# Modulation rows of a two-block transformer: loads on another queue, products in pairs, three vectors in other stages

## The chip, the cores and the metric

The kernel runs on one core of one Trainium2 chip. The metric is the device time of one execution in microseconds (us), as the median of several runs. A profile is one execution, recorded by the hardware.

## The reference

One launch computes two transformer blocks in a row on 256 tokens of width 1024, in float32. The first block has two layers, each with a mixer (differential attention and a gated recurrence in layer 0, attention in layer 1), layer norms, a feed-forward of width 4096 and a gated side input. The second block has two layers that are conditioned on a vector c, and carries a second stream of 256 context tokens with its own conditioning vector. For each of its layers six modulation vectors are computed for both streams, and they scale, shift and gate the normalised activations:

```
mod = (s_lat @ w_mod[i] + b_mod[i])[:, None, :]
mod_c = s_ctx @ w_mod[i] + b_mod[i]
sh1, sc1, g1, sh2, sc2, g2 = jnp.split(mod, 6, axis=-1)
h = rms_norm_2(x, norm_mix[i]) * (1.0 + sc1) + sh1
y, yc = token_mixers(h, hc, ...)
x = x + g1 * y
h = rms_norm_2(x, norm_ffn[i]) * (1.0 + sc2) + sh2
x = x + g2 * swiglu(h, w_gate[i], w_up[i], w_down[i])
```

Here `s_lat` and `s_ctx` are two vectors of 1024, and `w_mod[i]` is 1024 x 6144. None of this depends on the first block, so the twelve vectors (six for each of two layers, written j = 0 to 5 below) can be computed at any time before they are needed.

## The kernel before

All large weights are streamed once. `WeightStream` (L200 on) cuts them into units, mostly of 512 KB. For each unit SyncE (SP) issues a load into one of four raw buffers (L212), ACT rounds it to a high part (L214), DVE subtracts to get a low part (L216), and TensorE (PE) multiplies three times (high by high, high by low, low by high; L279 to L281 in `proj`, L825 to L827 and L850 to L852 in the feed-forwards of the first block, L1474 to L1476 in those of the second). There are four buffers for the two parts too, and a unit's load is emitted four units ahead of its use.

The program is a list of items, each a number of weight units and a function. It is put together by `weave`, which spreads one list evenly over another, and `side_by_side`, which puts side work at the ends of feed-forward groups. So side work such as the context stream and the modulation rows runs between weight products. The items are traced in this order; a scheduler then orders the instructions of each engine, by priority (the place in the program) and by a simulated time, and allots the buffers and PSUM banks. Each engine, and each queue of DMA issues, executes in that fixed order and waits at an instruction whose inputs or buffers are not ready. SP has the weight loads and most others; POOL (GpSimd) has the modulation rows, small parameters, and the reciprocal square roots of the norms (L385).

`modulation` (L938) makes one item of each quarter of a vector (`part(j, u)`, u from 0 to 3). A quarter takes two rows of 128 x 1024 of `w_mod_2`, 512 KB each. POOL issues the row's load (L952) into a buffer `fr` (two of them; `bc` for the first six rows), and PE multiplies it by the silu of the two conditioning vectors, `cT` (128 x 32, two columns of which are used), in four column groups of 32 that lie side by side in the array (L954). The eight rows of a vector accumulate in the one PSUM bank `fil`. With the last quarter DVE clears a buffer, POOL loads the bias into it, and DVE adds the sum (L962); gates are kept as they are, and the others are turned into columns by two small products (L968).

Of the kernel before, what the change touches and what calls it, by code (L numbers as in the profile page):

```python
# [119 lines left out]
def body(ctx: ExitStack, tc: tile.TileContext, A: dict, out: bass.AP):  # L120
# [29 lines left out]

    mm = nc.tensor.matmul
    V = nc.vector
    S = nc.scalar
# [114 lines left out]
    def proj(w, kdim, chunks, xs, evac, t_outer=(), tag="acc", first=0):  # L268
        new = tag if callable(tag) else lambda: PT(tag)

        items = []

        nu = kdim // 2

        def mms(o, x, wt, u):
            (xh, xl), (wh, wl) = x, wt
            for kk in range(2):
                k = 2 * ((u + first) % nu) + kk
                mm(o, xh[:, k, :], wh[:, kk, :], start=(u == 0 and kk == 0), stop=False)  # L279
                mm(o, xh[:, k, :], wl[:, kk, :], start=False, stop=False)  # L280
                mm(o, xl[:, k, :], wh[:, kk, :], start=False, stop=(u == nu - 1 and kk == 1))  # L281

        for ci, (c0, n) in enumerate(chunks):
            units = [(w, 2 * ((u + first) % nu), 2, c0, n) for u in range(nu)]
            if ci in t_outer:
                def whole(*wts, ci=ci, n=n):
                    for i, x in enumerate(xs()):
                        ps = new()[:, 0:n]
                        for u in range(nu):
                            mms(ps, x, wts[u], u)  # L290
                        evac(ci, i, ps)

                items.append((units, whole))
            else:
                held = []
                for u in range(nu):
                    def part(wt, ci=ci, n=n, u=u, held=held):
                        x = xs()
                        if u == 0:
                            held.extend(new()[:, 0:n] for _ in x)  # L300
                        for i in range(len(x)):
                            mms(held[i], x[i], wt, u)
                        if u == nu - 1:
                            for i in range(len(x)):
                                evac(ci, i, held[i])

                    items.append(([units[u]], part))
        return items

    def projT(w, kdim, c0, nb, xs, evac, tag="acc"):  # L310
# [4 lines left out]
        def part(wt, u):  # L315
# [3 lines left out]
            for kk in range(2):  # L319
                k = 2 * u + kk  # L320
                mh, ml = [m[:, k, :] for m in xT]
                for b in range(nb):
# [3 lines left out]
                    mm(o, wh[:, kk, bs], ml, start=False, stop=False, skip_group_check=True)  # L326
                    mm(o, wl[:, kk, bs], mh, start=False, stop=(k == kdim - 1), skip_group_check=True)
            if 2 * u == kdim - 2:
# [460 lines left out]
    def block1_layer(l, xT, done, side):  # L789
# [25 lines left out]
        def up_part(g, u, wt):  # L815
# [3 lines left out]
            for b in range(4):  # L819
                o = pss[g][b // 2][:, b % 2, :]  # L820
                for kk in range(2):
# [4 lines left out]
                    mm(o, wh[:, kk, bs], ml, start=False, stop=False, skip_group_check=True)  # L826
                    mm(o, wl[:, kk, bs], mh, start=False, stop=(k == 7), skip_group_check=True)  # L827
            if u == 3:
# [9 lines left out]
        def down_part(g, hs, *us):  # L838
# [3 lines left out]
            for t in range(2):  # L842
                ts_ = slice(t * P, (t + 1) * P)
                for n in range(2):
                    o = acc[g][t][n]
                    for i, h in enumerate(hs):
                        wh, wl = us[2 * i + n]
                        for kk in range(2):
                            b = 2 * h + kk
                            mm(o, hh[:, b, ts_], wh[:, kk, :], start=(b == 0), stop=False)  # L850
                            mm(o, hh[:, b, ts_], wl[:, kk, :], start=False, stop=False)  # L851
                            mm(o, hl[:, b, ts_], wh[:, kk, :], start=False, stop=(b == 3))  # L852
                    if 1 in hs:
# [84 lines left out]
    def modulation(l, box, js):  # L938
# [3 lines left out]
        def part(j, u):  # L942
# [3 lines left out]
            if u == 0:  # L946
                st[j] = PT("fil")
            ps = st[j]
            for k in (2 * u, 2 * u + 1):
                early[0] += 1  # L950
                raw = T([P, D], F32, "bc" if early[0] <= 6 else "fr", 2)
                nc.gpsimd.dma_start(raw, A["w_mod_2"][l, k * P:(k + 1) * P, j * D:(j + 1) * D])  # L952
                for g in range(4):
                    mm(ps[32 * g:32 * g + 32, 0:256], cT[:, k, :], raw[:, 256 * g:256 * g + 256],  # L954
                       start=(k == 0), stop=(k == KD - 1), tile_position=(0, 32 * g))
            if u < 3:
                return
# [461 lines left out]
    def block2_layer(l, xT, pr, box, ce, done, side):  # L1419
# [44 lines left out]
        def up_part(g, m, u, wt):  # L1464
# [3 lines left out]
            for b in range(2):  # L1468
                o = pss[g][m][:, b, :]
                bs = slice(b * P, (b + 1) * P)  # L1470
                for kk in range(4):
# [3 lines left out]
                    mm(o, wh[:, kk, bs], ml, start=False, stop=False, skip_group_check=True)  # L1475
                    mm(o, wl[:, kk, bs], mh, start=False, stop=(k == 7), skip_group_check=True)  # L1476
            if m == 1 and u == 1:
# [8 lines left out]
        def down_part(gs, *us):  # L1486
# [5 lines left out]
            for t in range(2):  # L1492
                ts_ = slice(t * P, (t + 1) * P)
                for n in range(2):
                    cs = slice(n * 512, (n + 1) * 512)
                    o = acc["y"][t][n]
                    for i, (g, (hh, hl)) in enumerate(zip(gs, hs)):
                        wh, wl = us[2 * i + n]
                        for kk in range(2):
                            mm(o, hh[:, kk, ts_], wh[:, kk, :], start=(kk == 0 and g == 0), stop=False)  # L1500
                            mm(o, hh[:, kk, ts_], wl[:, kk, :], start=False, stop=False)  # L1501
                            mm(o, hl[:, kk, ts_], wh[:, kk, :], start=False, stop=(kk == 1 and g == NG - 1))  # L1502
                    if NG - 1 in gs:
# [22 lines left out]
    def ctx_ffn(box):  # L1526
# [16 lines left out]
        def up_part(g, m, u, wt):  # L1543
# [3 lines left out]
            for b in range(2):  # L1547
                o = pss[g, m][:, b, :]
                bs = slice(b * P, (b + 1) * P)
                for kk in range(4):  # L1550
# [3 lines left out]
                    mm(o, wh[:, kk, bs], ml, start=False, stop=False, skip_group_check=True)  # L1554
                    mm(o, wl[:, kk, bs], mh, start=False, stop=(k == 7), skip_group_check=True)
            if u == 0:
# [11 lines left out]
        def down_part(g, *us):  # L1568
# [3 lines left out]
            for t in range(2):  # L1572
                ts_ = slice(t * P, (t + 1) * P)
                for n in range(2):
# [3 lines left out]
                    for kk in range(2):  # L1578
                        mm(o, h[:, 0, kk, ts_], wh[:, kk, :], start=(kk == 0), stop=False)
                        mm(o, h[:, 0, kk, ts_], wl[:, kk, :], start=False, stop=False)  # L1580
                        mm(o, h[:, 1, kk, ts_], wh[:, kk, :], start=False, stop=(kk == 1))
                    if g == 0:
# [80 lines left out]
    def mod(l, *js):  # L1663
        return modulation(l, boxes[l], js)

    program += block1_layer(0, xTs[0], to_next(1), dict(tail=flat(ctx_a[:1]), lr=4, mix=mod(0, 0, 1) + ctx_n + mod(0, 2), first=flat(ctx_a[1:2]) + mod(0, 3), ffn=ctx_a[2:-2],
                                                        end=flat(ctx_a[-2:]), last=mod(0, 4)))
    program += block1_layer(1, xTs[1], to_next(2), dict(tail=[], lr=6, mix=mod(0, 5) + mod(1, 0), first=mod(1, 1), ffn=ctx_b[:-2],
                                                        end=flat(ctx_b[-2:]), last=mod(1, 2)))
    ce1 = Stream(1)  # L1670
# [59 lines left out]
```

The twelve vectors lie in the program as follows (the calls at the end of `body`): j = 0, 1, 2 of layer 0 in the mixer of the first block's layer 0, j = 3 in the first group of its feed-forward, j = 4 at the end of that layer; j = 5, and j = 0 of layer 1, in the mixer of the first block's layer 1, j = 1 in the first group of its feed-forward, j = 2 at the end of the layer; j = 3 and 4 in the mixer of the second block's layer 1, j = 5 between its output projection (two quarters) and its feed-forward (two quarters). In the profile the mixers' last parts are found at 130 to 160 and 600 to 640, the first block ends at about 938, the second block's last mixer runs to about 1690, and its last feed-forward from 1726.

## Time and profile before

| | us |
|---|---|
| median of 3 runs | 1928.41 |
| lowest and highest | 1926.06, 1931.02 |
| profiled execution, its own time | 1929.02 |
| span of that execution in the trace | 1927.3 |

The profile gives, for each engine, its busy time and what it waited for. An engine's idle time is put down to the instruction before which it was idle, and to what ended the wait. A name such as `PE fil L954 <- DMA fr<-in_w_mod_dram` reads: TensorE, about to write `fil` at line 954, waited for the transfer into buffer `fr`. In a timeline, neighbouring instructions of one line are merged, with their count behind "x"; every float32 matmul here is two instructions, so that a row's four products are 8. PEclk is the granted share of TensorE's clock. A few matmul records can be missing.

### The profile page before, as it was taken

How to read it: one execution, taken by the hardware profiler on the slowest of the kernel's cores; microseconds unless marked ns; L12 is line 12 of the kernel's file. 1: busy time of each engine (PE TensorE's matmuls, PEld its weight loads, DVE VectorE, ACT ScalarE, POOL GpSimd, SP SyncE). 2: the span in 40 equal slices, each digit the busy share in tenths (PEclk: the TensorE clock that was granted, in tenths of full speed). 3: DMA queues.
4: the chain of work that ended last, by engine and by line, in shares of the span. 5: the costliest groups of instructions: out<-in, count | busy, mean ns of one | idle time of the engine just before them, and what ended most of it. 6: DMA issues, size and time to landing. Idle time of an engine off the chain costs nothing. (4 is left out here: it accounts for less than half of the span.)

```text
span 1927.3 us, 31895 instructions
## 1 busy us (share of the span) xinstructions
PE 1853.6 (96%) x12481; PEld 1578.1 (82%) x12481; DVE 1213.4 (63%) x2297; ACT 989.4 (51%) x1630; POOL 118.1 (6%) x194
## 2 busy tenths in 40 slices
PE   8989999999999999999899999999999999889997
PEld 5756797997887698887687998989998987669997
DVE  5564656557666666667577776676645766755555
ACT  5453465444556455553457753454646556444443
POOL 3111100000101100000000000000000000210000
PEclk9998999999999999999899999999999999899999
DMA  8744653555576554556452445556565454455553
GB/s 296 248 169 149 232 186 131 184 166 202 186 231 217 178 184 139 168 183 206 135 186 92 133 141 165 176 185 186 183 186 169 138 181 137 139 190 183 185 180 105
DMA packets 101411, 338.84 MB, mean 176 GB/s; under 512 B 12148, under 2 KB 13388, under 8 KB 101260
## 3 DMA queue, kind: packets, MB, share of 16 engines
q1 hardware_dynamic: 86124, 286.00, 46.1%
q0 software_dynamic: 15136, 50.80, 7.8%
q8 instruction: 98, 1.61, 0.3%
q14 instruction: 53, 0.43, 0.1%
HBM read 335.70 MB, written 1.05 MB: 175 GB/s over the span
## 5 line engine op out<-in xcount | busy, mean ns | idle before, releaser
L216 DVE TENSOR_TENSOR wl<-wr,wh 128x1024 fp32r<-128x1024 f32 (+3 forms) x562 | 637.9, 1137 | 398.9 <-ACT wh L214 395.9
L214 ACT CAST wh<-wr 128x1024 fp32r<-128x1024 f32 (+3 forms) x562 | 549.5, 980 | 645.3 <-PE acc L281 140.1
L279 PE MATMUL acc<-wh,mh 128*128 128x256 f32 (+3 forms) x400 | 133.0, 338 | 0.3 <-ACT mh L357 0.2
L280 PE MATMUL acc<-wl,mh 128*128 128x256 f32 (+3 forms) x400 | 131.6, 330 | 0.5 <-DVE wl L216 0.5
L281 PE MATMUL acc<-wh,ml 128*128 128x256 f32 (+3 forms) x400 | 131.2, 330 | 0.0
L280 PE MATMUL acc<-wl,xh 128*128 128x512 f32 (+3 forms) x304 | 119.3, 393 | 2.4 <-DVE wl L216 2.4
L279 PE MATMUL acc<-wh,xh 128*128 128x512 f32 (+3 forms) x304 | 117.6, 397 | 2.9 <-ACT xh L378 1.9
L281 PE MATMUL acc<-wh,xl 128*128 128x512 f32 (+3 forms) x304 | 117.1, 386 | 0.1
L850 PE MATMUL acc<-wh,a 128*128 128x512 f32 x256 | 101.9, 401 | 0.0
L852 PE MATMUL acc<-wh,a 128*128 128x512 f32 x256 | 101.3, 397 | 0.0
L851 PE MATMUL acc<-wl,a 128*128 128x512 f32 x256 | 101.3, 396 | 0.0
L1476 PE MATMUL sc<-xh,wl 128*128 128x256 f32 x352 | 99.6, 283 | 0.0
L1475 PE MATMUL sc<-xl,wh 128*128 128x256 f32 x352 | 99.5, 283 | 0.0
L1474 PE MATMUL sc<-xh,wh 128*128 128x256 f32 x352 | 99.5, 283 | 0.0
L1475 PE MATMUL sc<-ml,wh 128*128 128x256 f32 x352 | 99.2, 282 | 0.0
L1474 PE MATMUL sc<-mh,wh 128*128 128x256 f32 x352 | 98.5, 280 | 0.0
L1476 PE MATMUL sc<-mh,wl 128*128 128x256 f32 x352 | 98.4, 280 | 0.0
L952 POOL DMA_DIRECT2D fr<-in_w_mod_dram x90 | 48.8, 544 | 690.5 <-PE fil L954 563.3
L279 PEld LDWEIGHTS acc<-wh,mh 128*128 128x128 f32 x400 | 75.5, 190 | 13.7 <-issue 4.5
L954 PE MATMUL fil<-fr,cT 128*32 128x256 f32 x720 | 66.4, 415 | 19.5 <-DMA fr<-in_w_mod_dram 19.5
L280 PEld LDWEIGHTS acc<-wl,mh 128*128 128x128 f32 x400 | 75.9, 190 | 7.7 <-DVE wl L216 1.4
L281 PEld LDWEIGHTS acc<-wh,ml 128*128 128x128 f32 x400 | 75.6, 190 | 6.3 <-issue 0.6
(575 smaller groups left out, 4764.4 us busy)
## 6 DMA issues: line engine op xcount, KB each, us to landing
wr<-in_ffn_w_dram SPq DMA_DIRECT2D x128, 512.0 KB, 3.4
fr<-in_w_mod_dram POOLq DMA_DIRECT2D x90, 512.0 KB, 5.1
wr<-in_w_gate_dram SPq DMA_DIRECT2D x66, 512.0 KB, 3.9
wr<-in_w_up_dram SPq DMA_DIRECT2D x66, 512.0 KB, 4.1
wr<-in_w_down_dram SPq DMA_DIRECT2D x66, 512.0 KB, 3.6
wr<-in_w_in_dram SPq DMA_DIRECT2D x40, 384.0 KB, 3.1
wr<-in_ev_w_in_dram SPq DMA_DIRECT2D x28, 512.0 KB, 4.6
wr<-in_w_in_dram SPq DMA_DIRECT2D x28, 512.0 KB, 4.1
```

What stands on the lines that cost most here:

```text
L214: S.copy(hi, raw)
L216: V.tensor_tensor(lo, raw, hi, ALU.subtract)
L279: mm(o, xh[:, k, :], wh[:, kk, :], start=(u == 0 and kk == 0), stop=False)
L280: mm(o, xh[:, k, :], wl[:, kk, :], start=False, stop=False)
L281: mm(o, xl[:, k, :], wh[:, kk, :], start=False, stop=(u == nu - 1 and kk == 1))
L850: mm(o, hh[:, b, ts_], wh[:, kk, :], start=(b == 0), stop=False)
L851: mm(o, hh[:, b, ts_], wl[:, kk, :], start=False, stop=False)
L852: mm(o, hl[:, b, ts_], wh[:, kk, :], start=False, stop=(b == 3))
L954: mm(ps[32 * g:32 * g + 32, 0:256], cT[:, k, :], raw[:, 256 * g:256 * g + 256], start=(k == 0), stop=(k == KD - 1), tile_position=(0, 32 * g))
L1474: mm(o, wh[:, kk, bs], mh, start=(k == 0 and b == 0), stop=False, skip_group_check=True)
L1475: mm(o, wh[:, kk, bs], ml, start=False, stop=False, skip_group_check=True)
L1476: mm(o, wl[:, kk, bs], mh, start=False, stop=(k == 7), skip_group_check=True)
```

## The change

The loads of rows and biases are issued by SP in place of POOL. The two rows of a quarter are loaded first and then multiplied together: in two rounds over the four column groups, the rows alternate, so that each group gets both rows and the first product needs the second row. Each quarter is its own accumulation, which DVE adds to the bias row; the bias row is cleared and loaded with the first quarter. All dense weight products that end a triple now go through `wm`, which records the last one issued, and a quarter's products get an ordering edge behind it (`tc.issue_after`, an edge for the scheduler, not a wait on the chip). Three vectors move: j = 4 of layer 0 into the feed-forward of the first block's layer 1, j = 2 of layer 1 into that of the second block's layer 0, j = 5 of layer 1 into that of the second block's layer 1, from its fifth group of items on. The diff, without the further places at which `mm` becomes `wm`:

```
+    dense = []
+
+    def wm(*args, **kw):
+
+        dense[:] = [mm(*args, **kw).ins]
...
-                mm(o, xl[:, k, :], wh[:, kk, :], start=False, stop=(u == nu - 1 and kk == 1))
+                wm(o, xl[:, k, :], wh[:, kk, :], start=False, stop=(u == nu - 1 and kk == 1))
...
             if u == 0:
-                st[j] = PT("fil")
-            ps = st[j]
+                bm = st[j] = T([P, 256], F32, "gate" if j in (2, 5) else "bm", 3 if j in (2, 5) else 1)
+                V.memset(bm, 0.0)
+                for s in range(2):
+                    nc.sync.dma_start(bm[s:P:32, :], A["b_mod_2"][l, j * D:(j + 1) * D].rearrange("(g n) -> g n", g=4))
+            bm, ps = st[j], PT("fil")
+            raws = {}
             for k in (2 * u, 2 * u + 1):
                 early[0] += 1
-                raw = T([P, D], F32, "bc" if early[0] <= 6 else "fr", 2)
-                nc.gpsimd.dma_start(raw, A["w_mod_2"][l, k * P:(k + 1) * P, j * D:(j + 1) * D])
-                for g in range(4):
-                    mm(ps[32 * g:32 * g + 32, 0:256], cT[:, k, :], raw[:, 256 * g:256 * g + 256],
-                       start=(k == 0), stop=(k == KD - 1), tile_position=(0, 32 * g))
+                raws[k] = T([P, D], F32, "bc" if early[0] <= 6 else "fr", 2)
+                nc.sync.dma_start(raws[k], A["w_mod_2"][l, k * P:(k + 1) * P, j * D:(j + 1) * D])
+            with tc.issue_after(dense[0]) if dense else nullcontext():
+
+                for rnd in range(2):
+                    for g in range(4):
+                        k = 2 * u + (g + rnd + 1) % 2
+                        mm(ps[32 * g:32 * g + 32, 0:256], cT[:, k, :], raws[k][:, 256 * g:256 * g + 256],
+                           start=(k % 2 != g % 2), stop=(k % 2 == g % 2), tile_position=(0, 32 * g))
+            V.tensor_tensor(bm, ps[:, 0:256], bm, ALU.add)
             if u < 3:
                 return
-            bm = T([P, 256], F32, "gate" if j in (2, 5) else "bm", 3 if j in (2, 5) else 1)
-            V.memset(bm, 0.0)
-            for s in range(2):
-                nc.gpsimd.dma_start(bm[s:P:32, :], A["b_mod_2"][l, j * D:(j + 1) * D].rearrange("(g n) -> g n", g=4))
-            V.tensor_tensor(bm, ps[:, 0:256], bm, ALU.add)
...
-            rest = dense[:16] + weave(dense[16:] + g, side["swa"][:8])
+            rest = dense[:16] + weave(dense[16:] + g, side["swa"])
...
-            prog += weave([do(gla_out, e, y)] + outp[1:], side["swa"][8:-2]) + side["swa"][-2:]
+            prog += [do(gla_out, e, y)] + outp[1:]
...
-                                                        end=flat(ctx_a[-2:]), last=mod(0, 4)))
+                                                        ffn=ctx_a[2:-2], end=flat(ctx_a[-2:]), last=[]))
...
-                                                        end=flat(ctx_b[-2:]), last=mod(1, 2)))
+                                                        ffn=weave(ctx_b[:-2], mod(0, 4)), end=flat(ctx_b[-2:]), last=[]))
...
-        "na": ffn_n, "swa": ffn_c, "pre": [], "from": 2, "ffn": [do(layer2_params, 1, prs[1])] + G(["norm", "kv", "znv", "gla"]), "end": L(["nk", "skv"])})
+        "na": ffn_n, "swa": ffn_c, "pre": [], "from": 2, "ffn": weave([do(layer2_params, 1, prs[1])] + G(["norm", "kv", "znv", "gla"]), mod(1, 2)), "end": L(["nk", "skv"])})
...
-        "swa": mod(1, 3, 4, 5), "from": 11, "ffn": [], "end": [],
+        "swa": mod(1, 3, 4), "from": 2, "ffn": mod(1, 5), "end": [],
```

## Rows read from the trace of the kernel before

**Rows 1.** The page's first part: busy time, share and instructions by engine.

```profile
PE 1853.6 (96%) x12481; PEld 1578.1 (82%) x12481; DVE 1213.4 (63%) x2297; ACT 989.4 (51%) x1630; POOL 118.1 (6%) x194
```

**Rows 2.** Waits of PE (us, times, longest): whole span; 930 to 950; 1700 to 1735.

```profile
PE fil L954 <- DMA fr<-in_w_mod_dram: 19.5, 10, 4.2
...
PE fil L954 <- DMA fr<-in_w_mod_dram: 4.8, 2, 4.2
...
PE fil L954 <- DMA fr<-in_w_mod_dram: 4.9, 4, 2.8
```

**Rows 3.** By stretch, L954 alone: length, PE and PEld busy, PEclk, DMA share, GB/s.

```profile
130.00:160.00 30.00, 5.16 (x48) 1.08 (x48) 0.69 0.53 178
...
600.00:680.00 80.00, 8.52 (x80) 2.49 (x80) 0.90 0.63 209
...
938.10:949.40 11.30, 3.18 (x30) 0.80 (x30) 0.75 0.66 203
...
1630.00:1690.00 60.00, 10.69 (x128) 3.23 (x128) 0.91 0.41 136
...
1713.00:1726.10 13.10, 3.60 (x40) 0.83 (x40) 0.87 0.82 305
...
sum 1266.00, PE 69.83 PEld 20.34; mean PE 5.82 PEld 1.70
```

**Rows 4.** Timeline of PE at four places: start, length, instruction, count, wait before it.

```profile
23.92 0.39 PE L280 MATMUL acc<-wl,xh 128*128 128x512 f32 x1
24.24 1.07 PE L954 MATMUL fil<-bc,cT 128*32 128x256 f32 x16
25.24 0.50 PE L281 MATMUL acc<-wh,xl 128*128 128x512 f32 x1
...
42.82 0.64 PE L954 MATMUL fil<-bc,cT 128*32 128x256 f32 x8
...
176.38 0.62 PE L954 MATMUL fil<-fr,cT 128*32 128x256 f32 x2
...
1730.22 0.64 PE L954 MATMUL fil<-fr,cT 128*32 128x256 f32 x8 [0.65 <-DMA fr<-in_w_mod_dram]
```

**Rows 5.** Timelines of POOL, ACT, PE and DVE at the first block's end.

```profile
939.08 1.04 POOL L952 DMA_DIRECT2D fr<-in_w_mod_dram  x2 [10.93 <-PE fil L954]
940.14 0.57 POOL L385 TENSOR_TENSOR stb<-sta,mhalf 128x1 f32<-128x1 f32 x1
...
943.90 1.15 ACT L378 CAST xh<-t 128x512 fp32r<-128x512 f32 x2
...
949.37 0.72 PE L279 MATMUL acc<-wh,xh 128*128 128x416 f32 x1
...
949.51 0.42 DVE L962 TENSOR_TENSOR gate<-fil,gate 128x256 f32<-128x256 f32 x1 [2.80 <-PE fil L954]
```

**Rows 6.** Timelines of ACT and PE where the last feed-forward starts.

```profile
1725.64 0.62 ACT L378 CAST xh<-t 128x512 fp32r<-128x512 f32 x1 [0.23 <-DVE t L377]
...
1726.07 0.39 PE L1474 MATMUL sc<-xh,wh 128*128 128x256 f32 x1
```

**Rows 7.** DMA issues: queue, count, size, median us to landing.

```profile
fr<-in_w_mod_dram POOLq DMA_DIRECT2D x90, 512.0 KB, 5.1
...
fr<-in_na_bias_dram SPq DMA_DIRECT2D x6, 512.0 KB, 4.5
```

**Rows 8.** Waits of SP's queue and of ACT over the whole span.

```profile
SPq L212 <- DVE wl L216: 1327.5, 463, 34.3
...
ACT wh L214 <- DMA wr<-in_ev_w_in_dram: 8.8, 6, 1.9
```

**Rows 9.** By stretch, all: length, PE, PEld, DVE, ACT, POOL busy, PEclk, DMA.

```profile
950.00:965.00 15.00, 12.98 (x54) 11.93 (x53) 5.68 (x12) 5.61 (x11) 0.55 (x1) 0.75 0.24 74
1250.00:1500.00 250.00, 250.00 (x1703) 230.33 (x1703) 156.13 (x192) 136.74 (x177) 3.56 (x4) 1.00 0.58 180
```

More of the change, by code (lines that the diff above doesn't have):

```diff
@@ L1 @@
 import math
+from contextlib import nullcontext
 from contextlib import ExitStack
@@ L326, in part @@
                     mm(o, wh[:, kk, bs], ml, start=False, stop=False, skip_group_check=True)
-                    mm(o, wl[:, kk, bs], mh, start=False, stop=(k == kdim - 1), skip_group_check=True)
+                    wm(o, wl[:, kk, bs], mh, start=False, stop=(k == kdim - 1), skip_group_check=True)
             if 2 * u == kdim - 2:
@@ L826, in up_part @@
                     mm(o, wh[:, kk, bs], ml, start=False, stop=False, skip_group_check=True)
-                    mm(o, wl[:, kk, bs], mh, start=False, stop=(k == 7), skip_group_check=True)
+                    wm(o, wl[:, kk, bs], mh, start=False, stop=(k == 7), skip_group_check=True)
             if u == 3:
@@ L851, in down_part @@
                             mm(o, hh[:, b, ts_], wl[:, kk, :], start=False, stop=False)
-                            mm(o, hl[:, b, ts_], wh[:, kk, :], start=False, stop=(b == 3))
+                            wm(o, hl[:, b, ts_], wh[:, kk, :], start=False, stop=(b == 3))
                     if 1 in hs:
@@ L1475, in up_part @@
                     mm(o, wh[:, kk, bs], ml, start=False, stop=False, skip_group_check=True)
-                    mm(o, wl[:, kk, bs], mh, start=False, stop=(k == 7), skip_group_check=True)
+                    wm(o, wl[:, kk, bs], mh, start=False, stop=(k == 7), skip_group_check=True)
             if m == 1 and u == 1:
@@ L1501, in down_part @@
                             mm(o, hh[:, kk, ts_], wl[:, kk, :], start=False, stop=False)
-                            mm(o, hl[:, kk, ts_], wh[:, kk, :], start=False, stop=(kk == 1 and g == NG - 1))
+                            wm(o, hl[:, kk, ts_], wh[:, kk, :], start=False, stop=(kk == 1 and g == NG - 1))
                     if NG - 1 in gs:
@@ L1554, in up_part @@
                     mm(o, wh[:, kk, bs], ml, start=False, stop=False, skip_group_check=True)
-                    mm(o, wl[:, kk, bs], mh, start=False, stop=(k == 7), skip_group_check=True)
+                    wm(o, wl[:, kk, bs], mh, start=False, stop=(k == 7), skip_group_check=True)
             if u == 0:
@@ L1580, in down_part @@
                         mm(o, h[:, 0, kk, ts_], wl[:, kk, :], start=False, stop=False)
-                        mm(o, h[:, 1, kk, ts_], wh[:, kk, :], start=False, stop=(kk == 1))
+                        wm(o, h[:, 1, kk, ts_], wh[:, kk, :], start=False, stop=(kk == 1))
                     if g == 0:
@@ L1664, in mod @@
         return modulation(l, boxes[l], js)
-    program += block1_layer(0, xTs[0], to_next(1), dict(tail=flat(ctx_a[:1]), lr=4, mix=mod(0, 0, 1) + ctx_n + mod(0, 2), first=flat(ctx_a[1:2]) + mod(0, 3), ffn=ctx_a[2:-2],
-                                                        end=flat(ctx_a[-2:]), last=mod(0, 4)))
-    program += block1_layer(1, xTs[1], to_next(2), dict(tail=[], lr=6, mix=mod(0, 5) + mod(1, 0), first=mod(1, 1), ffn=ctx_b[:-2],
-                                                        end=flat(ctx_b[-2:]), last=mod(1, 2)))
+    program += block1_layer(0, xTs[0], to_next(1), dict(tail=flat(ctx_a[:1]), lr=4, mix=mod(0, 0, 1) + ctx_n + mod(0, 2), first=flat(ctx_a[1:2]) + mod(0, 3),
+                                                        ffn=ctx_a[2:-2], end=flat(ctx_a[-2:]), last=[]))
+    program += block1_layer(1, xTs[1], to_next(2), dict(tail=[], lr=6, mix=mod(0, 5) + mod(1, 0), first=mod(1, 1),
+                                                        ffn=weave(ctx_b[:-2], mod(0, 4)), end=flat(ctx_b[-2:]), last=[]))
     ce1 = Stream(1)
```

## The prediction

> **What bounds the kernel now.** I read the page's engine shares first. TensorE is busy for 1853.6 of 1927.3 us [rows 1]; the other engines stand far below, so time is won only where TensorE idles or works inefficiently. The list of TensorE's own waits comes next: its largest entry is the product of the modulation rows (L954) waiting for its row to arrive, 19.5 us in 10 waits, of which 4.8 lie at the end of the first block's second layer (930 to 950) and 4.9 around the start of the last feed-forward (1700 to 1735) [rows 2]. Third, the table by stretch, restricted to L954: the 96 rows of modulation weights hold TensorE for 69.8 us [rows 3]. So they cost 69.8 + 19.5 = 89.3 us. Fourth, the timeline, to see what one row should cost. Two rows in one go (16 matmuls) took 1.07 us, one row (8) took 0.64, and a piece of one row, 2 matmuls, took 0.62 [rows 4]: the price hangs on the number of uninterrupted blocks more than on their length. The product behind a block is also longer, 0.50 against 0.39 [rows 4]. I counted 80 blocks, the first at 24.24 and the last at 1730.22 [rows 4], where 48 pairs would do.
>
> **The change, part by part.**
>
> *Pairs, queued behind a product.* The four column groups' matmuls now alternate between the two rows of a pair, and the first of them needs the row that is loaded last, so that a pair starts whole or not at all; the ordering edge keeps it from being placed ahead of its turn among the weight products. Nothing is added on TensorE: 768 matmuls stay. 48 x 1.07 = 51.4 us, against 89.3 with the waits: 37.9 less, if no pair waits. Blocks fall from 80 to 48, and 32 x (0.50 - 0.39) = 3.5 us goes with them. Together 41.4 at most.
>
> *What of that is not on the path.* At the first layer end the rows hold 3.18 us and wait 4.8 [rows 2, 3], 8.0 together. The next weight product started at 949.37, but its input was being cast by ACT from 943.90, two casts in 1.15 us [rows 5], so it could have started at about 944.5: 4.9 is released, 3.1 was hidden anyway. At the second one, 1713 to 1726.1, rows and waits take 3.60 + 4.3 (the 4.9 without the 0.65 at 1730.22) = 7.9 [rows 2, 3, 4]. Here the first feed-forward product at 1726.07 follows the last cast of its input, which began at 1725.64 [rows 6]: the normalisation chain sets this start, and all 7.9 was free. The other 9.8 of the 19.5 lies mostly in three stretches with many small products (130 to 160, 600 to 680, 1630 to 1690). They hold 5.16 + 8.52 + 10.69 = 24.4 us of L954 [rows 3], 34.2 with the waits; the 16 pairs in them (256 of the 768 matmuls) would take 17.1. That is 17.1 less, but attention and the gated mixers there hand small results between engines, and a TensorE released early from one wait may just meet the next. Between none and all I take half, since these stretches show both kinds of wait: 8.5 hidden. So 41.4 - 3.1 - 7.9 - 8.5 = 21.9.
>
> *Moving three vectors into feed-forwards.* Twelve pairs go where TensorE never pauses (250.00 of 250 us in the stretch from 1250, [rows 9]): each of their 1.07 us is fully paid there. This is already in the 51.4. What the boundaries lose is a filler, priced among the rivals. Four pairs in a feed-forward of some 190 us or more leave tens of us between them, so the rows are there long before.
>
> *SyncE's queue.* 96 row loads and 24 small bias loads leave POOL and go in among the weight loads. POOL gets 120 issues of about 0.5 us back. One of them stood on the path: at the first layer end two issues ran from 939.08 for 1.04 us, and the norm's reciprocal root began right behind, at 940.14 [rows 5]. I take 1.0 for that, and nothing elsewhere. On SP every row load now waits for its buffer (the pair before it must be multiplied), and the weight loads behind it wait too. The cover is the lead of the weight stream: four raw and four split buffers. It shows in the waits: SP stood 1327.5 us waiting for DVE to free a raw buffer, while ACT's casts waited only 8.8 us for a weight to land in their largest such entry [rows 8]. So I cost this at nothing; if the lead is used up, each late weight load stops TensorE, which is the slow rival. Landing gets no shorter in my sum: the rows on POOL's queue took 5.1 us in the median, a load of the same 512 KB on SP's 4.5 [rows 7], 0.6 that matters only where a pair waits. The Trainium skill (DMA: Bandwidth & Descriptors, "Issuing engines are not separate DMA queues") says that DMAs of all issuers run on the same DMA engines and that a further issuing engine saves only issue time. By that rule a new queue alone ends no wait, and up to 9.8 us, the waits away from the layer ends, would stay: 1916.
>
> *DVE.* Each pair is now added to the bias row by itself: 48 adds instead of 12, 36 x 0.42 [rows 5] = 15.1 us. DVE is busy 156.1 of 250 us in the feed-forward stretch [rows 9], and nobody waits for these sums until the vector is complete; I take 0, and 15.1 is the other bound. In return the one "fil" bank is free after every pair instead of after eight rows; no row prices that either way, and I leave it at nothing, between a small gain and one add's 0.42 us of delay for whoever wants the bank next. The bias rows' clearing and loads move from the end of a vector to its beginning, ahead of the products: covered.
>
> **Sum.** 21.9 + 1.0 = 22.9 us less. The profiled execution took 1929.0 us (span 1927.3), 0.6 above the median of 1928.4, which I neglect: 1929 - 23 = **1906 us**.
>
> **Rivals.**
>
> *The clock takes part of it back (1917 us).* After the waits at the first layer end the profile grants 0.75 of the clock from 950 to 965 [rows 9], and 0.69 from 130 to 160 [rows 3]: a mix of full speed and the half level, 1.2 GHz, after TensorE had idled. A boundary without its filler idles more steadily, whereas now rows run in the middle of the idle time. 0.25 x 15 = 3.7 us is what one such stretch loses; at three boundaries 11, so 1906 + 11 = 1917. For it: the falls above. Against it: they happened with the rows there, and because of waits that the change removes. The Trainium skill (TensorE: Matmul & The Clock Gate, "Why this matters for your kernels") asks for no idle gaps between bursts of matmuls, which speaks against taking work out of the boundaries; the trace agrees that idling there is followed by a lower clock.
>
> *The waits come back (1929 us, no change).* A pair can't start on its first row. If pairs are placed in TensorE's order earlier than their rows really land, each loses about the 0.5 us by which the second load follows the first (half of the 1.04 that two issues took, [rows 5]): 48 x 0.5 = 24, the whole gain. It is also what I'd see if pairs were split up and the blocks stayed near 80. For it: ten waits today show that the order, fixed at build time, counts on earlier landings than the chip gives. Against it: most of those waits come where several rows follow each other with nothing between them, and that is what the change ends at two places.
>
> *SyncE starves the weights (1953 us, slower).* Weight loads stand behind a row load whose buffer isn't free. Where pairs follow each other at every weight unit (the first feed-forward group of each layer, the two mixers), SP is held for a pair's spacing, the lead of the weight stream shrinks, and casts and products wait. At 1 us for each of the 48 pairs this gives 1906 + 48 = 1953; it turns the result slower than before from 0.6 us a pair on. For it: SP is in order and waits most of the time. Against it: SP's waits are for buffers freed late, not for missing data, and a cast waits for weights almost nowhere [rows 8].
>
> **How the numbers follow.** Forecast (1888 to 1920) 0.55. Clock, within the upper part of that and a little beyond, 0.10. All of the hidden parts gained too, under 1888, 0.06. Waits back, within 0.3%, 0.13. SyncE, slower, 0.16. Faster is 0.55 + 0.10 + 0.06 = 0.71. A measurement of this kernel can tell some 0.3%, 5.8 us, from no change. For the range: everything gained gives 1929 - 41.4 - 1.0 = 1887, and the stretch at 0.69 back at full clock another 0.31 x 30 = 9 at most, so 1880 as the low end; upward it takes in the clock, the 15.1 of DVE and the waits that come back, to 1932. Beyond it lies most of the slow rival.
>
> **What would show it.** Right: L954 in about 48 blocks of 16 matmuls, some 1.07 us each and near 51 us in all; its wait for rows down from 19.5 to a few us; the first product after the second layer's end some 5 us earlier relative to the last product before it; the start of the last feed-forward still behind its casts, with nothing gained; feed-forwards longer by 4.3 us each (four pairs). Wrong: casts (L214) waiting for weights by tens of us, SP waiting for L954 in front of weight loads, or a sum of L954's waits that is again near 20. A clock well under 1.00 in the stretches after the three boundaries would show the first rival.

## The result: 15 us slower, and the profile after

The changed kernel took 1943.9 us in the median (1942.5 to 1950.5), the kernel before 1928.9 beside it: a ratio of 1.0084, with a 95% interval of 1.0064 to 1.0104. The forecast was 1906 us, with a range up to 1932. The profiled execution took 1943.0, its span is 1940.9.

The new line numbers: the rows' products are now L969 (L954 before), their loads L963, the columns' products L979, and the last product of a weight triple shows as L157 everywhere. The engine shares of the page:

```profile
PE 1844.7 (95%) x12481; PEld 1585.8 (82%) x12481; DVE 1224.9 (63%) x2333; ACT 989.5 (51%) x1630; POOL 52.6 (3%) x74
```

Beside [rows 1], TensorE is busy for 8.9 us less, in a span that is 13.6 longer. Its idle time (span less busy) rose from 73.7 to 96.2. The list of its waits, whole span (us, times, longest):

```profile
PE sc L184 <- DVE a L1008: 11.8, 3, 4.5
PE fil L969 <- DMA fr<-in_w_mod_dram: 6.4, 3, 2.6
PE sm L184 <- DMA t<-in_p_dram: 6.2, 3, 3.0
```

Before, the first and the third of these read:

```profile
PE sc L177 <- DVE a L997: 3.8, 3, 2.2
...
PE sm L177 <- DMA t<-in_p_dram: 2.1, 2, 1.7
```

The wait for rows fell from 19.5 [rows 2] to 6.4, as forecast. So other idle time grew by 22.5 + 13.1 = 35.6 us. Next, L969 alone by stretch (columns as in [rows 3]):

```profile
0.00:1941.00 1941.00, 56.24 (x768) 20.85 (x768) 0.97 0.54 175
...
197.00:245.00 48.00, 4.28 (x64) 1.67 (x64) 0.96 0.71 232
600.00:680.00 80.00, 3.21 (x48) 1.25 (x48) 0.89 0.54 180
936.00:951.00 15.00, 0.00 (x0) 0.00 (x0) 0.77 0.17 52
1380.00:1510.00 130.00, 4.28 (x64) 1.67 (x64) 1.00 0.63 196
...
1717.00:1734.00 17.00, 0.00 (x0) 0.00 (x0) 0.65 0.38 123
1780.00:1890.00 110.00, 4.28 (x64) 1.67 (x64) 1.00 0.63 206
```

The rows cost 56.24 + 6.4 = 62.6 us, against 89.3: 26.7 less. But they have left the places where TensorE waits: nothing is left between 936 and 951 or between 1717 and 1734, three pairs instead of five between 600 and 680 [rows 3], and whole vectors stand in feed-forwards, at 197 to 245, 1380 to 1510 and 1780 to 1890. There each pair is paid in full. What TensorE does now at the three places, and what a pair costs in the last feed-forward (timeline of PE; here and below, lines in between are left out):

```profile
644.13 0.66 PE L184 MATMUL sm<-ident,t 128*128 128x128 f32 x2 [2.98 <-DMA t<-in_p_dram]
657.15 1.87 PE L184 MATMUL sc<-ident,x 128*128 128x128 f32 x8 [3.44 <-DVE ml L365]
661.32 0.58 PE L832 MATMUL sc<-mh,wh 128*128 128x256 f32 x1 [2.31 <-DVE ml L365]
...
700.30 0.51 PE L979 MATMUL fil<-cst,bm 128*128 128x8 f32 x4
703.07 0.38 PE L184 MATMUL fil<-ident,cgy 128*128 128x128 f32 x2
706.31 0.44 PE L184 MATMUL fil<-ident,cgy 128*128 128x128 f32 x2 [2.86 <-DVE xl L365]
707.67 0.70 PE L1241 MATMUL fil<-ck,c 64*128 64x256 f32 x2 [0.92 <-DVE xl L365]
709.68 0.79 PE L1241 MATMUL sm<-ck,c 64*128 64x256 f32 x1 [1.32 <-ACT t L1261]
...
1723.41 1.97 PE L184 MATMUL sc<-ident,a 128*128 128x128 f32 x8 [3.58 <-DVE a L1008]
1729.92 1.94 PE L184 MATMUL sc<-ident,a 128*128 128x128 f32 x8 [4.53 <-DVE a L1008]
...
1782.06 1.07 PE L969 MATMUL fil<-fr,cT 128*32 128x256 f32 x16
1783.06 0.38 PE L1485 MATMUL sc<-xh,wh 128*128 128x256 f32 x1
```

Before, j = 1 of layer 1 ran between 622 and 670, its columns' product came at 670.88, and the context stream's small products on the same bank `fil` (`cgy`, then `ck,c`) stood scattered among weight products:

```profile
670.88 0.52 PE L968 MATMUL fil<-cst,bm 128*128 128x8 f32 x4
675.33 0.63 PE L177 MATMUL fil<-ident,cgy 128*128 128x128 f32 x2
...
690.35 0.38 PE L177 MATMUL fil<-ident,cgy 128*128 128x128 f32 x2
...
699.07 0.70 PE L1230 MATMUL fil<-ck,c 64*128 64x256 f32 x2
```

Now this vector runs from 668.06 on, inside the feed-forward; its columns come at 700.30, and the small products follow in a chain, one behind the other, with 2.86 + 0.92 + 1.32 us of idle time. The granted clock fell as well. Both kernels, all instructions by stretch (columns as in [rows 9]), first before, then after:

```profile
640.00:680.00 40.00, 36.31 (x198) 25.06 (x197) 29.50 (x51) 17.36 (x31) 7.54 (x12) 0.93 0.72 244
680.00:720.00 40.00, 40.00 (x284) 36.75 (x284) 23.40 (x34) 22.84 (x35) 0.00 (x0) 0.99 0.54 171
```

```profile
640.00:680.00 40.00, 30.81 (x191) 25.83 (x190) 23.01 (x38) 16.91 (x29) 3.92 (x4) 0.79 0.55 180
680.00:720.00 40.00, 34.90 (x230) 28.83 (x230) 22.18 (x42) 16.57 (x30) 0.00 (x0) 0.91 0.55 193
```

In these 80 us TensorE is 10.6 us longer idle, and the clock fell from 0.93 to 0.79 and from 0.99 to 0.91.

Where the whole loss arises shows when the same weight unit's cast (ACT, L214 before and L221 now) is looked up in both traces:

| cast starts, before | after | later by |
|---|---|---|
| 570.43 | 559.53 | -10.90 |
| 744.59 | 744.29 | -0.30 |
| 970.29 | 964.40 | -5.89 |
| 1356.98 | 1351.14 | -5.84 |
| 1553.56 | 1556.64 | 3.08 |
| 1604.27 | 1604.50 | 0.23 |
| 1745.04 | 1753.64 | 8.60 |
| 1904.60 | 1918.03 | 13.43 |

The changed kernel is ahead for most of the time. It loses 10.6 us around j = 1 of layer 1, 8.9 where j = 2 of layer 1 now stands, 8.4 in the last mixer and 4.8 in the last feed-forward.

### The profile page after: what moved, and what is told of

Read it like the earlier page. It is cut to its first block, busy times and chain, and to the rows that moved or that the text cites. A ratio compares the mean times of both kernels' runs of the same rounds, so it can differ in the third digit from the quotient of the medians.

```text
span 1940.9 us, 31897 instructions
## 1 busy us (share of the span) xinstructions
PE 1844.7 (95%) x12481; PEld 1585.8 (82%) x12481; DVE 1224.9 (63%) x2333; ACT 989.5 (51%) x1630; POOL 52.6 (3%) x74
## 5 line engine op out<-in xcount | busy, mean ns | idle before, releaser
L221 ACT CAST wh<-wr 128x1024 fp32r<-128x1024 f32 (+3 forms) x562 | 549.6, 981 | 664.4 <-PE acc L157 263.1
L157 PE MATMUL acc<-wh,a 128*128 128x512 f32 x472 | 186.7, 397 | 0.0
L157 PE MATMUL sc<-xh,wl 128*128 128x256 f32 x608 | 172.9, 285 | 0.0
L157 PE MATMUL sc<-mh,wl 128*128 128x256 f32 x608 | 172.1, 283 | 0.0
L157 PE MATMUL acc<-wh,ml 128*128 128x256 f32 (+3 forms) x400 | 131.6, 330 | 0.0
L157 PEld LDWEIGHTS sc<-xh,wl 128*128 128x128 f32 x608 | 117.6, 193 | 0.1
L157 PEld LDWEIGHTS sc<-mh,wl 128*128 128x128 f32 x608 | 116.3, 191 | 1.4 <-issue 1.4
L157 PE MATMUL acc<-wh,xl 128*128 128x512 f32 (+3 forms) x304 | 116.5, 385 | 0.1
L157 PEld LDWEIGHTS acc<-wh,a 128*128 128x128 f32 x472 | 89.0, 188 | 21.7 <-issue 0.4
L857 PE MATMUL acc<-wh,a 128*128 128x512 f32 x256 | 102.0, 402 | 0.0
```

The source lines that it names most:

```text
L157: dense[:] = [mm(*args, **kw).ins]
L221: S.copy(hi, raw)
```

## The experiments

Fourteen kernels were run, each beside the kernel before; ratios are to that, with their 95% intervals. 0.1% is 1.93 us.

**One part of the change undone.** `no_edge` leaves out the ordering edge, `pool_queue` puts the loads of rows and biases back on POOL, `old_places` undoes the moves.

```diff
-            with tc.issue_after(dense[0]) if dense else nullcontext():
+            with nullcontext():
```

> The changed kernel (1943.9 us) without the ordering edge; queue, pairs and places stay. Theory 'filler': the edge pins each pair behind weight products and so takes it out of the places where TensorE waits for a normalisation or an attention step; without it some pairs go back there and the time falls by 5 us or more, to 1939 or less, with smaller TensorE waits around 641 to 710. Rival 'SyncE': the loss is in loads queued behind each other on SP; unchanged within 3 us. Rival 'feed-forward': the loss is in the three vectors' new places; unchanged within 3 us.

Measured: 1936.9 us, 1.0040 (1.0021 to 1.0060), 0.44% below the changed kernel.

```diff
...
-                nc.sync.dma_start(raws[k], A["w_mod_2"][l, k * P:(k + 1) * P, j * D:(j + 1) * D])
+                nc.gpsimd.dma_start(raws[k], A["w_mod_2"][l, k * P:(k + 1) * P, j * D:(j + 1) * D])
```

> The changed kernel with row and bias loads issued by POOL again; edge, pairs and places stay. 'SyncE': the small loads of p and the weight loads are no longer behind the rows, the 2.98 us waits for p before L184 go and the time falls by 8 us or more, to 1936 or less. 'Filler' and 'feed-forward': unchanged within 4 us, or a little slower, as rows on POOL land some 0.6 us later.

Measured: 1941.4 us, 1.0068 (1.0042 to 1.0095).

```diff
...
-                                                        ffn=ctx_a[2:-2], end=flat(ctx_a[-2:]), last=[]))
+                                                        ffn=ctx_a[2:-2], end=flat(ctx_a[-2:]), last=mod(0, 4)))
...
-                                                        ffn=weave(ctx_b[:-2], mod(0, 4)), end=flat(ctx_b[-2:]), last=[]))
+                                                        ffn=ctx_b[:-2], end=flat(ctx_b[-2:]), last=mod(1, 2)))
...
-        "swa": mod(1, 3, 4), "from": 2, "ffn": mod(1, 5), "end": [],
+        "swa": mod(1, 3, 4, 5), "from": 11, "ffn": [], "end": [],
```

> The changed kernel with all twelve vectors in their places of before; queue, pairs and edge stay. 'Feed-forward': the time falls by 10 us or more, to 1934 or less, since the twelve pairs in feed-forwards cost 1.2 us each there. 'Filler': it falls by about 5 us, as pairs can lie in the waits at the layer ends again, but only behind a weight product. 'SyncE': unchanged within 3 us.

Measured: 1940.3 us, 1.0059 (1.0032 to 1.0086). No part alone explains the loss; only the edge's removal gained more than its interval. The queue does not make the gaps near 647, 652 and 695: with the loads on POOL they stay.

**One part alone.** `moves_only` is the kernel before with the three vectors moved, single rows, no edge, loads on POOL.

> The kernel before (1928.9 us) with only the three vectors moved; POOL queue, single rows, no edge. 'Feed-forward': slower than before by 8 us or more, 1937 or above. 'Filler': slower by 3 to 8 us, since 12 pairs are paid in full in the feed-forwards and only about 5 us of waits at the first block's end are saved. 'SyncE': the same as before within 3 us or faster by up to 5 us.

Measured: 1962.5 us, 1.0172 (1.0147 to 1.0197), the slowest of all. In its timeline the rows of j = 4 of layer 0 run one behind another in the feed-forward:

```profile
757.71 1.08 PE L954 MATMUL fil<-fr,cT 128*32 128x256 f32 x8 [4.92 <-DMA fr<-in_w_mod_dram]
759.71 1.08 PE L954 MATMUL fil<-fr,cT 128*32 128x256 f32 x8 [0.91 <-DMA fr<-in_w_mod_dram]
```

The order packs single rows together where nothing holds them apart, two buffers can't feed eight rows in a row, and TensorE stops in a stage that never stopped before; the waits for rows come to 36.4 us. With pairs the same vector stays spread out even without the edge: in `no_edge` they stand at 717.5, 769.4, 813.1 and 859.6.

`sp_only` (the kernel before with its 120 loads on SP), `pairs_only` (pairs, added one by one, on POOL, no edge, old places), `pairs_sp` and `pairs_edge` fill in the table.

```diff
-                nc.gpsimd.dma_start(raw, A["w_mod_2"][l, k * P:(k + 1) * P, j * D:(j + 1) * D])
+                nc.sync.dma_start(raw, A["w_mod_2"][l, k * P:(k + 1) * P, j * D:(j + 1) * D])
```

> Before with the loads of rows and biases on SP and nothing else: single rows, no edge, old places. Theory 'SyncE': 1935 to 1950, since each row load waits for its buffer on the queue of the weights. Theory 'filler': 1925 to 1933, the waits for rows at the two layer ends stay about 19 us in all.

Measured: 1924.5 us, 0.9965 (0.9949 to 0.9981). SyncE's theory falls: the queue alone makes the kernel faster. 'Filler' misses as well, by little in the time, but it had left the waits for rows at about 19 us, and they fell to 14.8.

> Before with the rows multiplied in pairs and added pair by pair, and nothing else: POOL's queue, old places, no edge. Theory 'filler' (what the change loses, it loses because the edge takes pairs out of the places where TensorE waits; the pairs themselves are pure gain): rows cost 51 to 55 us busy as in the changed kernel, and the time is 1905 to 1920. Theory 'SyncE' (loads on SP hold up other loads): the same, 1905 to 1920, since POOL keeps them. Theory 'shared bank' (pairs make every part of a vector take and return the one bank fil, and a pair needs both rows, so the small side products that share fil wait more, whatever the queue or edge): 1930 to 1945, with idle time of 1 us and more in front of products on fil or of pairs.

Measured: 1924.5 us, 0.9968 (0.9953 to 0.9984), between the theories' windows. L969 over the whole span of this run, then its wait for rows:

```profile
0.00:1920.30 1920.30, 63.06 (x768) 22.48 (x768) 0.98 0.55 176
```

```profile
PE fil L969 <- DMA fr<-in_w_mod_dram: 17.5, 10, 3.7
```

Without the edge the pairs save 6.8 us of the rows' 69.83 [rows 3] and 2 of their wait. They run ahead of their turn into the attention's tail, partly in pieces again, and wait there. And in the last mixer the pairs lose half of what they had won: by the casts of the same weight units this run is 15.1 us ahead of the kernel before at 1604, and 6.9 at 1745. TensorE waits 6.6 us there for DVE's `a`, in place of 1.6. All thirteen kernels with pairs lose 5.4 to 14.8 us between these two units, whatever their queue, edge and places; single rows on SP (`sp_only`) lose 2.7. What makes this loss was not tried.

> As pairs_only, with the loads of rows and biases on SP. Theory 'SyncE': 5 to 10 us more than pairs_only, with the 128 KB load of p landing late before 650 and ACT's casts waiting more for weights. Theory 'filler': within 4 us of pairs_only.

Measured: 1930.5 us in the median, with executions from 1917.9 to 1937.8; 0.9983 (0.9956 to 1.0010), not told apart from `pairs_only`.

> As pairs_only, with the ordering edge. Theory 'filler': 6 to 12 us more than pairs_only, and the gaps of the changed kernel at the attention's end (640 to 670) and at the two ends of layers come back. Theory 'SyncE': within 4 us of pairs_only.

Measured: 1930.7 us, 0.9993 (0.9975 to 1.0012), 0.25% above `pairs_only`. The rows are down to 57.10 us in all, yet the time is longer. The load of `p` is late here too (2.53 us of waiting at 649.86), with the rows on POOL, so that wait isn't SyncE's doing.

**Where the edge costs.** In `pairs_edge` and `pairs_only` the same weight unit's cast stands at 688.4 and 683.5, and eight units later at 723.5 and 706.3: 12 us more go there, in the first group of the second feed-forward. Two kernels set the edge by place.

```diff
-            with tc.issue_after(dense[0]) if dense else nullcontext():
+            with tc.issue_after(dense[0]) if dense and (l, j) not in ((0, 3), (1, 1)) else nullcontext():
```

> pairs_edge without the edge on the two vectors that lie in the first group of a feed-forward: j = 3 of layer 0 and j = 1 of layer 1. Theory 'first groups' (the edge costs its time there: before, these rows ran ahead of the first feed-forward product, in the attention's tail and the norm's wait, and the context stream's small products, which need the same bank fil, ran right behind them; with the edge all of it lies among the feed-forward products, where TensorE then waits): the 12 us that pairs_edge loses against pairs_only between 683 and 738 are gone, j = 1 of layer 1 is complete before 670, and the time is 1919 to 1925. Theory 'edge as such' (each pair placed behind a product costs alike): two vectors of twelve come free, a sixth of the difference of 6, so 1929 to 1931.

Measured: 1921.3 us, **0.9948 (0.9930 to 0.9967)**, the fastest kernel of this study and faster than before. That is 0.45% below `pairs_edge`, for two vectors of twelve.

```diff
+            with tc.issue_after(dense[0]) if (l, j) in ((0, 3), (1, 1)) else nullcontext():
```

> pairs_only with the edge on j = 3 of layer 0 and j = 1 of layer 1 alone. Theory 'first groups': 10 to 14 us lost between 683 and 738 as in pairs_edge, with some 5 us of idle time before products on fil at about 700 to 715; in all 1928 to 1937. Theory 'edge as such': 1924 to 1926.

Measured: 1929.7 us, 0.9999 (0.9986 to 1.0012), 0.31% above `pairs_only`. The timelines of PE around the second feed-forward's start, `edge_not_first` first, then `edge_first_only`:

```profile
666.72 1.07 PE L969 MATMUL fil<-fr,cT 128*32 128x256 f32 x16 [1.56 <-DVE plms L916]
668.65 0.51 PE L979 MATMUL fil<-cst,bm 128*128 128x8 f32 x4
672.38 0.38 PE L184 MATMUL fil<-ident,cgy 128*128 128x128 f32 x2
687.95 0.38 PE L184 MATMUL fil<-ident,cgy 128*128 128x128 f32 x2
```

```profile
664.11 1.07 PE L969 MATMUL fil<-fr,cT 128*32 128x256 f32 x16
...
695.01 1.07 PE L969 MATMUL fil<-fr,cT 128*32 128x256 f32 x16
698.68 0.51 PE L979 MATMUL fil<-cst,bm 128*128 128x8 f32 x4
700.53 0.44 PE L184 MATMUL fil<-ident,cgy 128*128 128x128 f32 x2 [1.34 <-DVE mf L980]
702.36 0.44 PE L184 MATMUL fil<-ident,cgy 128*128 128x128 f32 x2 [1.40 <-DVE xl L365]
703.72 1.22 PE L1241 MATMUL fil<-ck,c 64*128 64x256 f32 x2 [0.92 <-DVE xl L365]
706.25 0.79 PE L1241 MATMUL sm<-ck,c 64*128 64x256 f32 x1 [1.32 <-ACT t L1261]
```

The first line of each is the vector's last pair in the one, its first in the other. Free, it ends in the norm's wait, the bank is handed on at 668.65, and 16 us lie between the two `cgy` products. Held back, it ends at 696, and the vector's columns and the context's products come as one chain over `fil`, with 1.34 + 1.40 + 0.92 + 1.32 = 5.0 us of idle time. The first of these waits is for the bank: DVE's `mf` (L980) reads the columns out of it. That the others follow from the one bank, and not from the order alone, was not tried with a second bank. The clock, by stretch, `edge_not_first` and then `edge_first_only`:

```profile
680.00:720.00 40.00, 40.00 (x289) 36.74 (x288) 24.83 (x35) 23.88 (x36) 0.00 (x0) 1.00 0.51 160
```

```profile
680.00:720.00 40.00, 35.03 (x221) 28.88 (x220) 20.78 (x37) 15.89 (x27) 3.23 (x6) 0.87 0.53 175
```

Only j = 1 of layer 1 shows this loss. By the casts behind the first group of layer 0 (at 349 in `pairs_only`), `edge_first_only` is 0.5 us and `pairs_edge` 0.1 us behind `pairs_only`, so there the edge at j = 3 cost next to nothing; and `edge_not_first`, which frees j = 3, is even 4.6 us behind `pairs_edge` at that point, as far as single traces tell.

> The changed kernel with the edge on the three moved vectors alone; all others are free to run ahead. Theory 'first groups' (edge costs its time at unmoved vectors around the starts of feed-forwards, and the moves cost by themselves, since a pair in a feed-forward is paid in full, about 1.2 us each, with what its old place had hidden): 1932 to 1938, like no_edge, with no loss of 11 us between 683 and 723. Theory 'feed-forward' (it is the edge that makes the moved pairs cost): 1940 to 1944.

This is the changed kernel with the edge on the moved vectors alone. Measured: 1938.1 us, 1.0041 (1.0023 to 1.0060), like `no_edge`: what the edge costs, it costs at the vectors that weren't moved.

**What the moves cost.** To `edge_not_first`, one kernel adds the moves of j = 4 of layer 0 and j = 2 of layer 1, the other that of j = 5 of layer 1 (the diffs are the change's own lines).

> edge_not_first with j = 4 of layer 0 and j = 2 of layer 1 moved as in the changed kernel, j = 5 of layer 1 in its old place. Theory 'places' (a pair in a feed-forward is paid in full, about 1.3 us each, and its old place gives little back, since there TensorE then waits for the norm's chain or for smaller things): 6 to 10 us more than edge_not_first, so 1927 to 1931, with the first layer's end no more than 5 us shorter. Theory 'edge' (the moves cost only with the edge at the first groups): within 3 us of edge_not_first.

Measured: 1933.5 us, 1.0015 (0.9998 to 1.0032), 0.67% (13 us, some 5 to either side) above `edge_not_first`, more than expected.

> edge_not_first with j = 5 of layer 1 moved as in the changed kernel, the other two in their old places. Theory 'places': four pairs of 1.21 us in the last feed-forward, 4.8 in all, and at the end of the mixer the normalisation chain sets the start with or without them, so 3 to 6 us more than edge_not_first, 1924 to 1927. Theory 'edge': within 2 us of edge_not_first.

Measured: 1928.6 us, 0.9992 (0.9971 to 1.0014), 0.44% (8.5 us, some 5.5 to either side) above, more than expected too. The profiled spans differ by 6.5, but 4.2 of that is no effect of the move: up to 1704 both traces have the same matmuls in the same order, and the cast at 1592.27 in `edge_not_first` stands at 1596.46 here. Two executions can differ by that much. The end of the last mixer in PE's timeline, `edge_not_first` first, then `cure_last_move`:

```profile
1708.23 1.09 PE L184 MATMUL sc<-ident,a 128*128 128x128 f32 x8 [2.22 <-DVE a L1008]
1714.67 1.94 PE L184 MATMUL sc<-ident,a 128*128 128x128 f32 x8 [4.35 <-DVE a L1008]
1718.80 1.94 PE L969 MATMUL fil<-fr,cT 128*32 128x256 f32 x16 [2.18 <-DMA fr<-in_w_mod_dram]
```

```profile
1712.30 1.97 PE L184 MATMUL sc<-ident,a 128*128 128x128 f32 x8 [3.60 <-DVE a L1008]
1718.80 1.94 PE L184 MATMUL sc<-ident,a 128*128 128x128 f32 x8 [4.53 <-DVE a L1008]
1722.25 0.80 PE L1485 MATMUL sc<-xh,wh 128*128 128x256 f32 x2 [1.51 <-ACT xh L385]
```

Taking the rows out gained little: the waits for DVE's `a` are longer, and the first eight transposes take 1.97 instead of 1.09 us. By the casts, the stretch around the mixer's end became 2.5 us shorter and the feed-forward 4.8 longer, so that these traces put the move at 2.3 us.

**A kernel that went another way.** `pairs_two_queues` is `pairs_only` with the second row of each pair on SP and the first on POOL.

```diff
-                nc.gpsimd.dma_start(raws[k], A["w_mod_2"][l, k * P:(k + 1) * P, j * D:(j + 1) * D])
+                (nc.sync if k % 2 else nc.gpsimd).dma_start(raws[k], A["w_mod_2"][l, k * P:(k + 1) * P, j * D:(j + 1) * D])
```

> pairs_only with the second row of each pair loaded on SP and the first on POOL. Theory 'landing' (a pair waits since two rows land one after the other on one queue, and the two buffers hold only one pair): the waits for rows, some 17 us in pairs_only, fall below 12, and the time is 1917 to 1922. Theory 'buffers' (the pair before it must be multiplied before either load can start, whatever the queue): waits of 15 to 19 us, 1922 to 1928.

Measured: 1943.5 us, 1.0068 (1.0038 to 1.0097), slower than either queue alone. The waits for rows rose to 25.9 us, the longest 7.2, so both theories miss. Pairs now start in pieces, for example two matmuls at 624.20 after 6.38 us of waiting: that the row loaded second is there no longer says that the other one is. Why the loads come that late wasn't tried.

## Why the prediction was wrong, step by step

**Pairs, right in kind, too large in size.** "48 x 1.07 = 51.4 us, against 89.3 with the waits" gave 37.9 and measured 26.7 in the changed kernel (56.24 + 6.4), most pairs whole and at 1.07 us. But wholeness came from the edge, not from the order of the products alone, which the prediction put as "a pair starts whole or not at all": without the edge the rows took 63.06 + 17.5 = 80.6. And a saving on rows was no saving of time in the last mixer, where all kernels with pairs fell back by 5 us or more, for which the sum has no term.

**What isn't on the path: the step that failed.** The prediction subtracts 3.1, 7.9 and 8.5 us, 19.5 in all, as what other waits hide, but it charges nothing for taking rows out of such waits. The ordering edge is free in its sum, moved pairs cost no more than the 1.07 us "already in the 51.4", and for the three stretches with many small products it lets the pairs keep half of their cover. The runs showed idle time in its place: away from the rows, TensorE idled 35.6 us longer. The two vectors of first feed-forward groups had run in the attention's tail and in the norm's wait, where they cost little. With the edge they lie among feed-forward products, and j = 1 of layer 1 delays the context's products on bank `fil` into one chain. Freed of the edge, the two give 0.45% (8.7 us), by the traces all of it at j = 1; in another setting (`edge_first_only`) they cost 0.31%, and in the changed kernel the unmoved vectors' edges cost 0.43%.

**Moved vectors: right in sign, too small.** That a pair is "fully paid there" held in the last feed-forward, which grew by 1.2 a pair. Elsewhere it was too little: set beside `edge_not_first` by casts, `cure_two_moves` loses 6.6 us over the four pairs of j = 4 of layer 0 and 8.9 over those of j = 2 of layer 1, where the prediction has 4.3 each; and the first block's end, put at 4.9 released, gave back 2.4. So its terms make a loss of some 4 for these two, and 13 was measured. Of the 8.9 (206.1 instead of 197.2 us between the same two weight units' casts), four pairs are 4.3, a wait on ACT's `mh` (1539.06) is 2.0, and the rest lies in slower neighbours. Some 4 us more appear in the last mixer; what makes them wasn't tried, and it is no more than two executions of the same order differed by. For the last move the prediction's terms make a loss of 4.3 us (7.9 hidden where it came from, four pairs paid), and the measured 8.5, with its interval, and the 2.3 of the traces leave that standing.

**"What the boundaries lose is a filler."** So the prediction said, and priced it only through the clock, at 11 us, with a chance of 0.10. This was the rival nearest to the truth, and its price was too low by the idle time itself. A lower clock is shown, but where the edge holds rows back: 0.87 instead of 1.00 between 680 and 720. Of the boundaries that lost their rows, only the last mixer's end shows it: 0.81 from 1698 to 1743, against 0.96 from 1690 to 1735 before. Behind the first block it is 0.77 (944 to 959) against 0.75. The Trainium skill (TensorE: Matmul & The Clock Gate, "Why this matters for your kernels") warns against idle gaps between bursts of matmuls. The trace agrees, with the transposes of 1.97 instead of 1.09 us behind the 3.60 us gap.

**SyncE's queue.** Costed at nothing, with the slow rival at 0.16. As priced, that rival is refuted: alone the queue gave 0.9965. But the term was not nothing. Casts waited 14.4 us for weights in their largest such entry, instead of 8.8 [rows 8], SP waited for row buffers ahead of weight loads, and TensorE waited longer for casts (before, then after):

```profile
PE acc L279 <- ACT wh L214: 0.6, 1, 0.6
```

```profile
SPq L963 <- PE fil L969: 101.9, 39, 8.1
...
PE acc L286 <- ACT wh L221: 4.1, 5, 1.7
```

With the loads back on POOL (`pool_queue`) the last entry is 1.4; 2.7 of the 4.1 lie in the first 31 us.

The prediction's sentence from the Trainium skill (DMA: Bandwidth & Descriptors, "Issuing engines are not separate DMA queues"), that a further issuing engine saves only issue time, would have let the waits for rows stand. Here they fell from 19.5 to 14.8 when nothing but the queue changed; whether by landing or by the new order isn't told apart. With pairs and edge, SP's part is open: 1.0059 in `old_places` against 0.9993 in `pairs_edge`, while the profiled spans, 1933.0 and 1931.1, hardly differ.

**DVE.** Taken as 0. It is busy 11.5 us more, and the longest wait of TensorE on a pair's sum (L971) is 0.90 us, at 607.33. Right as far as that goes. But an add also stands in DVE's work ahead of `a` in the last mixer (0.41 us at 1710.15 in `pairs_only`), for which TensorE waits; what the adds cost there isn't told apart.

**In sum**, in parts of the time before: pairs -0.32%, edge on all vectors +0.25%, the moves +0.67% and +0.44% (measured on `edge_not_first`) make +1.04%; the changed kernel measured +0.84%. The terms come from runs with intervals of 0.15 to 0.3% to either side and need not add exactly. Another chain of runs, each with one part more, divides the 0.84 otherwise: pairs -0.32, edge +0.25 (`pairs_edge`), SP's queue +0.66 (`old_places`), moves +0.25. In it the queue is the largest loss and the moves are within the noise, while undoing the queue in the changed kernel gave only 0.16. So that the edge costs is shown; how the rest divides between the moves and SP's queue is open. `edge_not_first` with its loads on SP wasn't tried.

## What to carry to other kernels

Work that fills waits is priced by where it runs, not by its busy time: look up each block's place in the trace before, and count a block that leaves a wait for a stage that never waits at its full length, with the idle time that it leaves behind. An edge that keeps such work from running ahead helps where it would be cut into pieces and harms where running ahead was free, so set it by place: with the edge off at the two first groups, no vector moved and the loads on POOL, the same pairs made the kernel faster than before (0.9948). Where side jobs share one PSUM bank, look at what stands behind the one that is delayed: here the next job's first product waited for the bank. And before a difference between two traces is given a cause, look how far they differ where their order is the same: here by 4 us.

## What was not expected of the hardware

The same eight transposes at the last mixer's end took 1.97 us behind a gap of 3.60 us and 1.09 behind one of 2.22, with rows of the moved vector at work ahead of it; the granted clock from 1690 to just behind the first feed-forward product (1724 and 1722) was 0.81 without these rows and 0.88 with them. Filler work may thus pay for itself in the clock of what follows; no run measured this alone. And splitting the two loads of a pair over two queues made the waits longer (25.9 us), though either queue alone gave less (17.5 on POOL, 14.9 on SP).
